# Token tiles shifted by 32 bytes in the partition, and three instead of four activation buffers in the down projection

## Chip, cores and metric

The kernel runs on one core of one Trainium2 chip. The metric is the device time of one execution in microseconds; of several executions the median counts.

## What is computed

A trunk of two layers over 256 tokens of width 1024. Each layer has a token mixer and then a retrieval over 16,384 single-neuron experts. The second part is what matters here:

```python
def peer_ffn(h, wq, keys, u_tab, v_tab):
    q = (h @ wq).reshape(b, s, PEER_HEADS, 2, PEER_HALF)
    sc = jnp.einsum('bshpd,hpnd->bshpn', q, keys)
    half_s, half_i = lax.top_k(sc, PEER_TOPK)
    ...
    gate = jax.nn.softmax(top_s, axis=-1)
        act = jax.nn.gelu(jnp.einsum('td,thkd->thk', hb, u_tab[eb]), approximate=False)
        return jnp.einsum('thk,thkd->td', gb * act, v_tab[eb])
```

The kernel does not gather the chosen experts. It computes the activations of all 16,384 experts (u, the up projection), multiplies them with a gate that is zero for experts not chosen, and multiplies the result with all of v (the down projection).

## The kernel before

**Products in parts.** Every fp32 operand is split into a high part (rounded to fp32r) and a low part (the rest), and a product is three matmuls: high by high, high by low, low by high.

**Weights.** All weight matrices pass through one stream (class `Stream`, lines 144 to 214) in pieces of 128 x 1024. A piece is loaded by SP into one of four `raw` tiles, and split in two halves of 512 columns into the rings `hi` and `lo` of three pieces. A split is of one of three kinds, chosen by shares that differ by stage: ACT rounds to `hi` (L199) and DVE subtracts to `lo` (L201); the same with POOL for the subtraction; or, the kind called dma here, ACT writes the negated rounding to `lo` (L195), POOL issues a DMA that adds `raw` onto it in memory (L196), and ACT writes `hi` (L197), all of it once for each half. A ring slot is written again when the matmuls of three pieces earlier have read it.

**Tokens.** The normalized tokens h stand in two tiles named `mid`, each 128 x (8 x 256) fp32r: `hhi` and `hlo`. `products` (L359 to L361, called for the query, up and some mixer projections) streams a 256-column row of them past 128 x 128 weights from `hi` and `lo`: 24 matmuls for one weight piece, 7,296 in the program (2,432 on each line). The up projection has 128 pieces in each layer. In the mixer's v, sv and su projections (L657 to L659) the roles are turned: a `mid` slice is the stationary operand, 192 matmuls in all. At three of the norms (`norm_mod`) the first four products run on another operand, `xparts`, which lies in a `big` tile: eight rows of 258 columns, one behind the other. The tile starts at a multiple of 64 bytes and a row is 1,032 bytes long, so row c starts 8c bytes past a multiple of 64, and row 4 starts 32 bytes past one. The 24 matmuls of a product go through the rows in order, three on each.

**Down.** `down` (L902) takes one v piece after another, chunk i of 128. `prep(i)` writes the high and low part of chunk i's activations into buffer i modulo 4 of a tile `ab` (ACT L910, DVE L911); then 12 matmuls (L925), with `ab` stationary and 512 columns of `hi` or `lo` moving. The third and fourth of them are the first to read `lo`: its first and its second half.

**Gates.** While up and down run, `gates` builds one-hot tiles `o1`, `o2`, `og` in fp16 and multiplies them (L876, 16 matmuls of 64 columns with `o1` stationary, 128 such groups); `o1` is stored to DRAM (`kept`) and read again.

**Order.** The program is written as a stream of work with a background scheduler that hands out slices by estimated costs; the framework then orders each engine's queue once more by data dependencies and buffers. In the course of the first layer's down projection DVE also runs 40 products with the next layer's modulation weights (L283), which wait for transfers of 512.5 KB (`wmod`).

The tiles `mid` and `xparts` are laid out by

```python
return self.one.tile([P, *shape], dt, name="mid", tag="mid", bufs=2)
n = NC * (T + 2)
self.xparts = [y[:, 8192 - (2 - i) * n:8192 - (1 - i) * n].rearrange("p (c t) -> p c t", c=NC) for i in range(2)]
```

Of the kernel before, what the change touches and what calls it, by code (L numbers as in the profile page):

```python
# [10 lines left out]
F32 = mybir.dt.float32  # L11
F32R = mybir.dt.float32r
# [6 lines left out]
P = 128  # L19
D = 1024  # L20
T = 256
# [195 lines left out]
class Trunk:  # L217
# [139 lines left out]
    def mm3(self, out, whi, wlo, hhi, hlo, start, stop):  # L357
        mm = self.nc.tensor.matmul
        mm(out, whi, hhi, start=start, stop=False)  # L359
        mm(out, whi, hlo, start=False, stop=False)  # L360
        mm(out, wlo, hhi, start=False, stop=stop)  # L361
# [539 lines left out]

    def down(self, acts):  # L902
        nc = self.nc
        ab = self.mid(4, 2, T, dt=F32R)
        self.acc = self.accs(4)

        def prep(i):
            src = acts[i // 32][:, i % 32]
            a = ab[:, i % 4]
            nc.scalar.activation(out=a[:, 0], in_=src, func=AF.Copy)  # L910
            nc.vector.tensor_tensor(out=a[:, 1], in0=src, in1=a[:, 0].bitcast(F32), op=ALU.subtract)  # L911

        for i in range(NK):
            if i % 64 == 0:
                prep(i)
                prep(i + 1)
            whi, wlo = self.weights()
            a = ab[:, i % 4]
            last = i == NK - 1
            terms = [(s, w, d) for s, w in ((0, whi), (0, wlo), (1, whi)) for d in range(2)]  # L920
            if last:
                terms.sort(key=lambda k: k[2])
            for tt in range(2):
                for s, w, d in terms:
                    nc.tensor.matmul(self.acc[2 * tt + d], a[:, s, P * tt:P * tt + P], w[:, 512 * d:512 * d + 512],  # L925
                                     start=i == 0 and s == 0 and w is whi, stop=last and s == 1)
            if i % 64 < 62:
                prep(i + 2)
            self.ahead()
            self.bg.pump(STEP)  # L930
            if i == 63:
                self.bg.finish()
                yield
        yield
# [83 lines left out]
    def start(self):  # L1018

        nc, io, one = self.nc, self.io, self.one  # L1020
        self.cols = one.tile([P, L * NCOL + 8], F32, name="cols")
        self.ident = one.tile([P, P], F32, name="ident")
        self.xT = one.tile([P, NC, T], F32, name="xT")
        self.ones = one.tile([P, P], F32, name="ones")
        self.eps = one.tile([P, 1], F32, name="eps")
        self.iota = one.tile([P, P, 2], FP16, name="iota")
        self.modT = one.tile([P, L, 48], F32, name="modT")
        self.idx = one.tile([P, 2, T], FP16, name="idx")
        self.gidx = one.tile([P, 2 * T], FP16, name="gidx")
        nc.vector.memset(self.ones, 1.0)  # L1030
        nc.vector.memset(self.eps, EPS)
        self.neghalf = one.tile([P, 8], F32, name="neghalf")
        nc.vector.memset(self.neghalf, -0.5)
        self.m = m = Carve(self.big(), self.big())
        self.m2 = Carve(self.big())
        row = m.take(D)
        nc.sync.dma_start(out=row[0:1], in_=io["crow"])
        nc.sync.dma_start(out=self.cols, in_=io["cols"])
        for i in range(2):
            nc.sync.dma_start(out=self.xT[:, 4 * i:4 * i + 4], in_=io["xT"][:, 4 * i:4 * i + 4])  # L1040
        cr = self.m2.take(D + 1)
        for i in range(2):
            b = self.bank()
            nc.tensor.matmul(b, self.ones[0:1], row[0:1, 512 * i:512 * i + 512], start=True, stop=True)
            nc.scalar.activation(out=cr[:, 512 * i:512 * i + 512], in_=b, func=AF.Silu)
        nc.vector.memset(cr[:, D:D + 1], 1.0)
        bufs = [self.m2.take(D + 1) for _ in range(6)]
        mods = self.mod_tiles(0, [j for c in range(NC) for j in (c, 8 + c)], cr, bufs, tail=False)
        next(mods)
        rs = self.rstd_d(m)  # L1050
        self.stream.depth = 0
        self.stream.share = {}
        self.stream.load(1)
        r = self.bias_rows()
        a = m.take(2, T)
        hhi, hlo = hb = [self.mid(NC, T, dt=F32R) for _ in range(2)]
        for c in range(NC):
            for _ in range(2 if c else 1):
                next(mods)
            sh, sc = self.modT[:, 0, c:c + 1], self.modT[:, 0, 8 + c:9 + c]  # L1060
            nc.vector.tensor_scalar(out=sc, in0=sc, scalar1=1.0, scalar2=self.col(0, c, 1), op0=ALU.add, op1=ALU.mult)
            t = a[:, c % 2]
            nc.vector.scalar_tensor_tensor(out=t, in0=self.xT[:, c], scalar=sc, in1=rs, op0=ALU.mult, op1=ALU.mult)
            nc.scalar.activation(out=hhi[:, c], in_=t, func=AF.Identity, bias=sh)  # L1064
            if c in (2, 4):
                self.stream.split(c // 2 - 1)
            nc.vector.scalar_tensor_tensor(out=hlo[:, c], in0=t, scalar=sh, in1=hhi[:, c].bitcast(F32), op0=ALU.add,  # L1067
                                           op1=ALU.subtract)
        for _ in mods:
            pass  # L1070
        self.stream.load(3)
        self.stream.depth = self.stream.RAW
        nc.sync.dma_start(out=self.ident, in_=io["consts"][:, 0:P])
        m.reset()
        self.bias = m.take(4, 256)
        self.table = self.bg.add(self.bias_table(r), rank=-1)
        self.bg.pump(0.1)
        self.mods = self.mod_tiles(0, list(range(16, 40)), cr, bufs[0:WBUFS])
        return hb
# [101 lines left out]
```

## Time and profile before

| | |
|---|---|
| median of 3 runs | 2026.73 us (2021.88 to 2034.16) |
| profiled execution, its own time | 2021.12 us |
| its span, first to last instruction | 2019.4 us |
| mean granted TensorE clock | 0.971 |
| PE busy | 1891.7 us (94%) |
| PEld (weight loads, beside PE) busy | 1711.1 us (85%) |
| DVE busy | 1472.8 us (73%) |
| ACT busy | 1130.2 us (56%) |
| POOL busy | 483.7 us (24%) |
| read from HBM | 388.72 MB |

Matmuls are pipelined and their ends are modelled, so the length of one in the trace is longer than the distance to the next. The distance from start to start is what is read here. A clock share of 1.00 is 2.4 GHz, 0.50 is 1.2 GHz.

### The profile page before, as it was taken

To read this page: it belongs to the slowest core of one execution; us is meant where nothing else is said; L and a number is where in the kernel's file an instruction comes from. 1 tells how busy PE (TensorE), PEld (TensorE's weight loads), DVE (VectorE), ACT (ScalarE), POOL (GpSimd) and SP (SyncE) were. 2 spreads that over 40 slices of the span, in tenths; PEclk is the share of its full clock that TensorE was granted. 3 is DMA by queue.
4 is the path that set the end of the run, shared out by engine and by line. 5 is a ranking of instruction groups with operands and counts; after the bars stand their busy time and mean duration, and the time that the engine had idled before them with its cause. 6 is when DMAs were issued, how large, how long until landed. Compare 5 with 4: busy or idle time off the path is not lost.

```text
span 2019.4 us, 37831 instructions
## 1 busy us (share of the span) xinstructions
PE 1891.7 (94%) x13718; PEld 1711.1 (85%) x13718; DVE 1472.8 (73%) x3360; ACT 1130.2 (56%) x2272; POOL 483.7 (24%) x432
## 2 busy tenths in 40 slices
PE   6887988999999999899998999998999999999998
PEld 4787988999999877678887899988999988888886
DVE  7888799677765887577668778954477668755555
ACT  4666543555555554455557676655555555565554
POOL 0122356751111111000001125877311111110001
PEclk7898998999999999899999999999999999999999
DMA  8987745767888888888557578887878888877674
GB/s 288 295 253 234 224 147 188 281 203 234 253 251 242 272 265 300 266 303 285 192 174 198 157 195 237 231 220 200 246 239 260 258 246 267 265 209 226 204 205 125
DMA packets 156958, 471.43 MB, mean 233 GB/s; under 512 B 17724, under 2 KB 19041, under 8 KB 156514
## 3 DMA queue, kind: packets, MB, share of 16 engines
q1 hardware_dynamic: 122786, 407.13, 58.7%
q0 software_dynamic: 33984, 61.88, 17.4%
q8 instruction: 107, 1.75, 0.3%
q14 instruction: 81, 0.66, 0.1%
HBM read 388.72 MB, written 18.36 MB: 202 GB/s over the span
## 4 chain that ended last, share of the span: by engine, by line
PE 63%; DMA 15%; DVE 11%; issue 6%; ACT 2%; POOL 2%; SPq 0%; POOLq 0%; DVEq 0%; ACTq 0%
PE acc L925 27%; PE bank L361 11%; PE bank L359 11%; PE bank L360 10%; DMA lo<-raw 10%; DMA big<-wmod 2%; DVE lo L201 2%; DMA raw<-v 2%; DVE big L283 2%; PE acc L876 1%; PE bank L876 1%; POOL lo L196 1%; DVE big L786 1%; POOL lo L201 1%; DVE big L787 1%
## 5 line engine op out<-in xcount | busy, mean ns | idle before, releaser
L199 ACT ACTIVATE hi<-raw 128x512 fp32r<-128x512 f32 x964 | 577.4, 624 | 366.3 <-PE bank L360 236.6
L361 PE MATMUL bank<-mid,lo 128*128 128x256 f32 x2432 | 700.2, 288 | 43.8 <-DMA lo<-raw 27.1
L359 PE MATMUL bank<-mid,hi 128*128 128x256 f32 x2432 | 702.5, 290 | 6.4 <-ACT mid L1064 5.9
L201 DVE TENSOR_TENSOR lo<-raw,hi 128x512 fp32r<-128x512 f32 x798 | 550.3, 714 | 212.5 <-ACT hi L199 207.6
L360 PE MATMUL bank<-mid,hi 128*128 128x256 f32 x2432 | 695.8, 286 | 0.8 <-DVE mid L1067 0.8
L925 PE MATMUL acc<-hi,mid 128*128 128x512 f32 x2048 | 570.3, 396 | 0.1
L361 PEld LDWEIGHTS bank<-mid,lo 128*128 128x128 f32 x2432 | 474.4, 195 | 51.9 <-DMA lo<-raw 31.6
L196 POOL DMA_DIRECT2D lo<-raw x236 | 203.9, 870 | 1175.5 <-ACT lo L195 851.1
L359 PEld LDWEIGHTS bank<-mid,hi 128*128 128x128 f32 x2432 | 473.4, 195 | 10.3 <-ACT mid L1064 7.0
L360 PEld LDWEIGHTS bank<-mid,hi 128*128 128x128 f32 x2432 | 474.2, 195 | 2.4 <-DVE mid L1067 2.0
L925 PEld LDWEIGHTS acc<-hi,mid 128*128 128x128 f32 x2048 | 386.2, 191 | 78.7 <-ACT mid L910 0.4
L925 PE MATMUL acc<-lo,mid 128*128 128x512 f32 x1024 | 326.0, 397 | 22.4 <-DMA lo<-raw 22.3
L201 POOL TENSOR_TENSOR lo<-raw,hi 128x512 fp32r<-128x512 f32 x166 | 261.8, 1652 | 97.5 <-ACT hi L199 88.7
L910 ACT ACTIVATE mid<-big 128x256 fp32r<-128x256 f32 x256 | 106.0, 416 | 303.1 <-PE acc L925 301.5
L925 PEld LDWEIGHTS acc<-lo,mid 128*128 128x128 f32 x1024 | 195.1, 191 | 71.9 <-DMA lo<-raw 31.0
L911 DVE TENSOR_TENSOR mid<-big,mid 128x256 fp32r<-128x256 f32 x256 | 107.9, 423 | 185.5 <-PE acc L925 144.5
L197 ACT ACTIVATE hi<-raw 128x512 fp32r<-128x512 f32 x236 | 147.5, 625 | 86.7 <-PE bank L360 54.9
L195 ACT ACTIVATE lo<-raw 128x512 fp32r<-128x512 f32 x236 | 146.6, 621 | 47.2 <-PE acc L925 44.7
L283 DVE SCALAR_TENSOR_TENSOR big<-big 128x1025 f32<-128x1025 f32 x96 | 122.3, 1281 | 35.0 <-DMA big<-wmod 26.8
L871 DVE TENSOR_TENSOR og<-o,gidx 128x512 f16<-128x512 f16 x256 | 96.5, 418 | 0.8 <-PE bank L876 0.4
L895 ACT ACTIVATE big<-bank 128x256 f32<-128x256 f32 x256 | 93.7, 366 | 0.0
L876 PEld LDWEIGHTS <-o 128*128 128x128 f16 x2048 | 67.3, 97 | 15.9 <-issue 13.1
(200 smaller groups left out, 1568.5 us busy)
## 6 DMA issues: line engine op xcount, KB each, us to landing
raw<-u SPq DMA_DIRECT2D x256, 512.0 KB, 4.8
raw<-v SPq DMA_DIRECT2D x256, 512.0 KB, 4.3
lo<-raw POOLq DMA_DIRECT2D x236, 256.0 KB, 5.1
big<-wmod SPq DMA_DIRECT2D x96, 512.5 KB, 6.4
raw<-win SPq DMA_DIRECT2D x40, 512.0 KB, 5.3
raw<-wq SPq DMA_DIRECT2D x32, 512.0 KB, 4.7
kept<-o SPq DMA_DIRECT2D x64, 256.0 KB, 4.9
o<-kept SPq DMA_DIRECT2D x64, 256.0 KB, 4.6
```

The lines of the kernel that those rows point to most:

```text
L195: nc.scalar.activation(out=lo, in_=raw, func=AF.Copy, scale=-1.0)
L196: nc.gpsimd.dma_start(out=lo, in_=raw, accum_op=ALU.add)
L197: nc.scalar.activation(out=hi, in_=raw, func=AF.Copy)
L199: nc.scalar.activation(out=hi, in_=raw, func=AF.Copy)
L201: eng.tensor_tensor(out=lo, in0=raw, in1=hi.bitcast(F32), op=ALU.subtract)
L283: nc.vector.scalar_tensor_tensor(out=w, in0=w, scalar=1.0, in1=sc, op0=ALU.mult, op1=ALU.mult, accum_out=self.modT[:, l, j:j + 1])
L359: mm(out, whi, hhi, start=start, stop=False)
L360: mm(out, whi, hlo, start=False, stop=False)
L361: mm(out, wlo, hhi, start=False, stop=stop)
L876: nc.tensor.matmul(b[:, 64 * j:64 * j + 64], o1[:, j // 2, :, j % 2], og[:, j // 2, s, :, j % 2], start=s == 0, stop=s == 1)
L911: nc.vector.tensor_tensor(out=a[:, 1], in0=src, in1=a[:, 0].bitcast(F32), op=ALU.subtract)
L925: nc.tensor.matmul(self.acc[2 * tt + d], a[:, s, P * tt:P * tt + P], w[:, 512 * d:512 * d + 512], start=i == 0 and s == 0 and w is whi, st ...
```

## The change

```diff
     def down(self, acts):
         nc = self.nc
-        ab = self.mid(4, 2, T, dt=F32R)
+        ab = self.mid(8 + 6 * T, dt=F32R)[:, 8:].rearrange("p (i s t) -> p i s t", i=3, s=2)
         self.acc = self.accs(4)
 
         def prep(i):
             src = acts[i // 32][:, i % 32]
-            a = ab[:, i % 4]
+            a = ab[:, i % 3]
...
             whi, wlo = self.weights()
-            a = ab[:, i % 4]
+            a = ab[:, i % 3]
...
         r = self.bias_rows()
         a = m.take(2, T)
+        one.tile([P, 8], F32, name="pad2")
         hhi, hlo = hb = [self.mid(NC, T, dt=F32R) for _ in range(2)]
```

`pad2` is never written or read. It is taken from the pool just before the first `mid` tile, and what is allocated later moves up by its 32 bytes a partition. In the built programs the two `mid` buffers go from bytes 201600 and 209792 of a partition to 201632 and 209824: from a multiple of 64 to 32 past one. `o1`, `o2` and `og` lie behind them and move in the same way (the first `o1` from 217984 to 218016). `hi`, `lo`, `raw`, `big` and all other tiles stay, at multiples of 64 for the four named. `ab` begins 8 words into its `mid` buffer, so that it is at a multiple of 64 again (201664 for the first), and has three buffers of 2 x 256 words instead of four.

With three buffers, `prep(i)` may write when the matmuls of chunk i - 3 have read, not those of chunk i - 4. The order on PE and POOL is the same in both programs. On ACT and DVE only rows of the down projection move, and on SP some loads of that time. The clearest place is a split of the dma kind. ACT before, at such a split in the second layer (`lo_64` and `hi_63` are the rings, `raw_21322` the piece, `mid` the tile of `ab`; names in brackets are semaphores of the engine or queue waited for):

```order
L910 ACTIVATE mid_18247<-big_15270 128x256 [waits PE_49]
L199 ACTIVATE hi_63<-raw_21302 128x512 [waits DMAHW6_49,DVE_49,PE_49]
L199 ACTIVATE hi_63<-raw_21302 128x512 [waits DVE_49,PE_49]
L195 ACTIVATE lo_64<-raw_21322 128x512 [waits DMAHW7_49,DVE_49,PE_49]
L197 ACTIVATE hi_63<-raw_21322 128x512 [waits PE_49,Activation_49]
L195 ACTIVATE lo_64<-raw_21322 128x512 [waits DVE_49]
L197 ACTIVATE hi_63<-raw_21322 128x512 [waits PE_49,Activation_49]
L910 ACTIVATE mid_18247<-big_15270 128x256
L910 ACTIVATE mid_18247<-big_15270 128x256 [waits PE_49]
```

ACT after, at the same split (the piece is now named `raw_21323`):

```order
L910 ACTIVATE mid_18248<-big_15271 128x256 [waits DVE_49,PE_49]
L199 ACTIVATE hi_63<-raw_21303 128x512 [waits DMAHW6_49,DVE_49,PE_49]
L199 ACTIVATE hi_63<-raw_21303 128x512 [waits DVE_49,PE_49]
L195 ACTIVATE lo_64<-raw_21323 128x512 [waits DMAHW7_49,DVE_49,PE_49]
L910 ACTIVATE mid_18248<-big_15271 128x256 [waits PE_49,Activation_49]
L197 ACTIVATE hi_63<-raw_21323 128x512 [waits PE_49,Activation_49]
L195 ACTIVATE lo_64<-raw_21323 128x512 [waits DVE_49]
L197 ACTIVATE hi_63<-raw_21323 128x512 [waits PE_49,Activation_49]
L910 ACTIVATE mid_18248<-big_15271 128x256 [waits DVE_49,PE_49]
```

A preparation that stood behind the whole split now stands between the first half's L195 and the second half's. This is so at 30 of the 32 dma splits of the two down projections.

DVE before, in the first layer's down projection where the modulation products (L283) run:

```order
L911 TENSOR_TENSOR mid_7446<-big_2081,mid_7446 128x256 [waits DVE_49,PE_49,Activation_49]
L283 SCALAR_TENSOR_TENSOR big_9589,modT_72<-big_9589 128x1025 [waits DMAHW1_49]
L201 TENSOR_TENSOR lo_64<-raw_9181,hi_63 128x512 [waits DMAHW6_49,Activation_49]
L201 TENSOR_TENSOR lo_64<-raw_9181,hi_63 128x512 [waits Activation_49]
L911 TENSOR_TENSOR mid_7446<-big_2081,mid_7446 128x256 [waits PE_49]
```

DVE after, at the same piece (now `raw_9182`):

```order
L283 SCALAR_TENSOR_TENSOR big_9590,modT_72<-big_9590 128x1025 [waits DMAHW7_49]
L291 SCALAR_TENSOR_TENSOR modT_72<-modT_72,cols_66 128x8
L911 TENSOR_TENSOR mid_7447<-big_2082,mid_7447 128x256 [waits PE_49,Activation_49]
L201 TENSOR_TENSOR lo_64<-raw_9182,hi_63 128x512 [waits DMAHW6_49,Activation_49]
L201 TENSOR_TENSOR lo_64<-raw_9182,hi_63 128x512 [waits Activation_49]
```

The preparation (L911) stood behind the split of a piece (L201, twice) and now stands ahead of it, and an L283, which waits for a transfer, is ahead of both.

## Rows read from the trace of the kernel before

**Rows 1.** The page's chain that ended last, shares of the span by line.
```profile
PE acc L925 27%; PE bank L361 11%; PE bank L359 11%; PE bank L360 10%; DMA lo<-raw 10%; DMA big<-wmod 2%; DVE lo L201 2%; DMA raw<-v 2%; DVE big L283 2%; PE acc L876 1%; PE bank L876 1%; POOL lo L196 1%; DVE big L786 1%; POOL lo L201 1%; DVE big L787 1%
```

**Rows 2.** By stage: length, busy us (count) of PE, PEld, DVE, ACT, POOL; clock; DMA; GB/s.
```profile
430.00:645.00 215.00, 213.59 (x2148) 211.75 (x2146) 142.59 (x295) 119.22 (x235) 33.86 (x37) 1.00 0.81 244
645.00:850.00 205.00, 187.44 (x1207) 148.71 (x1203) 157.74 (x350) 101.51 (x206) 20.64 (x24) 0.96 0.87 274
...
1400.00:1633.00 233.00, 230.19 (x2265) 228.47 (x2265) 142.87 (x299) 130.49 (x255) 49.39 (x51) 0.99 0.83 249
...
1800.00:2004.00 204.00, 202.68 (x888) 165.45 (x887) 113.03 (x200) 114.18 (x233) 14.32 (x17) 1.00 0.67 200
```

**Rows 3.** PE timeline, second layer's up: start us, length us, operation.
```profile
1451.82 0.65 PE L876 MATMUL acc<-og,o 128*128 128x64 f16 x16
1452.30 0.36 PE L359 MATMUL bank<-mid,hi 128*128 128x256 f32 x1
1452.50 0.28 PE L360 MATMUL bank<-mid,hi 128*128 128x256 f32 x1
...
1455.98 0.28 PE L359 MATMUL bank<-mid,hi 128*128 128x256 f32 x1
```

**Rows 4.** PE timeline, last product on `xparts` in the second layer's norm, and what follows.
```profile
1182.71 0.28 PE L359 MATMUL bank<-big,hi 128*128 128x258 f32 x1
...
1184.15 0.28 PE L359 MATMUL bank<-big,hi 128*128 128x258 f32 x1
...
1184.51 0.29 PE L359 MATMUL bank<-big,hi 128*128 128x258 f32 x1
...
1185.60 0.28 PE L359 MATMUL bank<-mid,hi 128*128 128x256 f32 x1
```

**Rows 5.** Groups by line, form and operation: busy us, mean ns | idle before.
```profile
L324 DVE SCALAR_TENSOR_TENSOR big<-xT,modT,big 128x256 fp32r<-128x256 f32 x24 | 12.9, 584 | 0.7 <-ACT big L323 0.6
...
L349 DVE SCALAR_TENSOR_TENSOR mid<-big,modT,mid 128x256 fp32r<-128x256 f32 x24 | 10.6, 482 | 1.8 <-ACT mid L348 1.5
```

**Rows 6.** ACT timeline at a dma split, second layer's down after its gates.
```profile
1821.67 0.42 ACT L910 ACTIVATE mid<-big 128x256 fp32r<-128x256 f32 x1 [1.26 <-PE acc L925]
1821.99 1.14 ACT L199 ACTIVATE hi<-raw 128x512 fp32r<-128x512 f32 x2
1824.16 0.63 ACT L195 ACTIVATE lo<-raw 128x512 fp32r<-128x512 f32 x1 [1.03 <-PE acc L925]
...
1825.22 0.62 ACT L195 ACTIVATE lo<-raw 128x512 fp32r<-128x512 f32 x1
```

**Rows 7.** POOL timeline: issue of that split's second half, and the last in the stage.
```profile
1826.13 0.86 POOL L196 DMA_DIRECT2D lo<-raw  x1 [0.18 <-issue]
...
1991.57 0.86 POOL L196 DMA_DIRECT2D lo<-raw  x1 [0.18 <-issue]
```

**Rows 8.** PE timeline there: two chunks' starts, and the wait for that half.
```profile
1818.75 1.07 PE L925 MATMUL acc<-hi,mid 128*128 128x512 f32 x4
...
1821.47 1.07 PE L925 MATMUL acc<-hi,mid 128*128 128x512 f32 x4
...
1831.18 0.50 PE L925 MATMUL acc<-lo,mid 128*128 128x512 f32 x1 [0.25 <-DMA lo<-raw]
```

**Rows 9.** PE's waits (us in total, times, longest): 760 to 870 us, then 1640 to 2000.
```profile
PE acc L925 <- DMA lo<-raw: 15.4, 11, 2.6
...
PE acc L925 <- DMA lo<-raw: 1.2, 4, 0.5
```

**Rows 10.** A piece of the chain in time order, first layer's down: start us, us.
```profile
824.28 8.55 DMA lo<-raw
```

**Rows 11.** Clock and PE timeline after a stall in the first layer's down.
```profile
814.40:816.50 2.10, 2.10 (x6) 1.65 (x5) 0.98 (x2) 0.00 (x0) 0.00 (x0) 0.50 0.67 185
...
814.42 1.91 PE L925 MATMUL acc<-hi,mid 128*128 128x512 f32 x4
816.13 0.91 PE L925 MATMUL acc<-lo,mid 128*128 128x512 f32 x2
```

## The prediction

> **What bounds the kernel now.** I read the chain of work that ended last first [rows 1]: the down matmuls hold 27% of it, the three lines of the token products 11, 11 and 10%, and the DMA that makes low parts 10%. The view by stage then says where PE sets the pace [rows 2]. In up it is busy 213.59 of 215 us and 230.19 of 233, so a nanosecond on each token matmul there is a nanosecond of the kernel. In the second layer's down it is 202.68 of 204. Only the first layer's down leaves PE idle for long, 187.44 of 205, with the DMA engines at a share of 0.87. So two things can move the time: the distance between PE's matmuls, and the waits in down.
>
> The distances come from the PE timelines, from start to start. A token matmul of 256 columns follows the last after 3.48 / 29 = 120.0 ns [rows 3]. A down matmul of 512 columns takes 2.72 / 12 = 226.7 ns [rows 8]. The 256 further columns cost 106.7 ns, so 13.3 ns of each fp32r matmul do not depend on its columns. All of it at a granted clock of 1.00, the level of 2.4 GHz.
>
> **Part 1: the moving operand of the token products at 32 past a multiple of 64.** There are 7,296 matmuls on L359, L360 and L361. The kernel before reads no `mid` row from such an address, but it reads `xparts` rows from eight offsets, the fifth of them exactly 32. One product of 24 such matmuls with 258 columns runs from 1182.71 to 1185.60 [rows 4], 120.4 ns each, where 120.0 and two columns at 0.417 ns would be 120.8. The three on row 4, at offset 32, take 0.36 us, 120 ns each. These reads also cross one boundary of 64 bytes more than an aligned row does, as the shifted tokens will, and pay nothing for it. I take 0 for this part. The average over the offsets is 0.4 ns below, which is 2.9 us over all; the three at offset 32 are read in steps of 10 ns, so 3 ns to either side of one, and 7,296 x 3 = 21.9 us is the bound in both directions.
>
> **Part 2: stationary operands at the new offset.** `o1` in the gates (2,048 matmuls, 0.48 us for 16, 30 ns each [rows 3]) and the 192 token slices of L657 to L659. No row of before shows a stationary operand of either type at offset 32. The nearest is the aligned one; I take 0, because 30 ns holds 26.7 for 64 columns and so little else that the load must lie beside other work. What it costs if it does not is the third rival. From below the bound is those 3.3 ns, 2,048 x 3.3 = 6.8 us. The Trainium skill ("TensorE: Matmul & The Clock Gate", section "Weight-path perf modes — Fast Weight Load (FWL) and DoubleRow") asks for 128 weights and a type other than FP32 for its fast load and names no address; by it nothing changes here either, and no run here shows it yet.
>
> **Part 3: writes of shifted tiles.** The low parts of tokens take DVE 482 ns each [rows 5]; the same operation into the shifting rows of `xparts` has a mean of 584. If all of that were the address, 32 operations (L349 24 times and 8 more in the first norm) would cost 32 x 0.10 = 3.3 us, on DVE, which has room. ACT's and DVE's work in down stays at its old offset. Stores and loads of `o1` start 32 bytes further on; their loads are issued a gate ahead. I take 0 for all of it.
>
> **Part 4: three buffers.** A preparation may now run two chunks ahead of its use, not three: 2 x 2.72 = 5.4 us [rows 8], of which it needs 0.42 on ACT and about as much on DVE. On plain chunks it stands where one stood before, ahead of the two L199 [rows 6]. That is covered. On DVE it now stands ahead of L201 and behind an L283 that waits for its transfer; that eats of the same 5.4 us, and is covered unless the transfer is some 4 us late.
>
> At 30 of the 32 dma splits it is not covered. The first half's L195 waits for the same matmul as before, so nothing is gained there. But the preparation now stands between it and the second half's L195, and ACT gives the next instruction 0.32 us after a preparation starts (1821.67 to 1821.99, [rows 6]). Queued behind it are L197, the second L195, POOL's second issue and the DMA. That L195 ends at 1825.84, POOL issues 0.29 us later [rows 6, 7], and the DMA lands just before 1831.18, where PE has waited 0.25 us for it [rows 8]. So this half comes 0.32 us later, and PE's wait becomes 0.57.
>
> How many of the 32 does it hit? The seven whose second halves are issued from 1826.13 to 1991.57 us [rows 7] have no gates to hide them: chunks of bare matmuls, and PE already waits at about half of them (four waits, 1.2 us, [rows 9]). 7 x 0.32 = 2.2 us. In the first layer, from 760 to 870 us, PE has 11 waits of 15.4 us together [rows 9], one or two at each of six splits; a second half takes up to 8.55 us to land there [rows 10] against 5.0 for the one in rows 7 and 8, so its bytes stand in full queues and a later start costs less than its delay. I take half, 6 x 0.16 = 1.0 us. The other 19 lie nearly all among gates, without such waits, and one gate's 0.48 us of PE time covers 0.32. Together 3.2 us; the ends are 0 and 32 x 0.32 = 10.2.
>
> **The sum.** 0 + 0 + 0 + 3.2 on the profiled execution's 2021.12 us (span 2019.4) gives 2024.3. That execution is 5.6 us below the median shown, so on the median it is 2026.7 + 3.2 = 2029.9 us, 0.2% slower. What a measurement of this kernel can tell from no change is about 0.5%, 10 us, so I call this no change.
>
> **The rivals.**
>
> *Faster: the shifted rows take away part of the 13.3 ns.* If the moving rows and the weights, both at multiples of 64 now, hold each other up at the change of weights, another offset frees it. Half of it is 7,296 x 6.65 = 48.5 us, 1978 us; all of it 97 us, 1930. For it speaks that the 13.3 ns is the same for 256 and 512 columns and so may belong to the change of weights, where both operands are read. Against it speak the three matmuls at offset 32 with 120 ns [rows 4]: half of the 13.3 would be 113. Chance 0.17. The Trainium skill (the same page, section "Back-to-back issue gap") gives N / 2.4 + 2.5 ns for a single matmul's gap, 109.2 ns for 256 columns; were that reached, an estimate from it is 10.8 x 7,296 = 79 us and a time of 1948. The trace disagrees with the formula for this type, by 120.0 to 109.2 here.
>
> *Slower: the late second half costs everywhere.* Place: the dma splits of both down projections. If the 19 others are as tight as the seven at the end, all 32 pay 0.32, 10.2 us. And a stall can lower the clock: after the one that ended just before 814.4 us the granted clock is 0.50, the level of 1.2 GHz, and matmuls follow after 1.71 / 4 = 0.43 us instead of 0.23 [rows 11]. If each of the first layer's six brings another 2.1 us at half clock, that is 6 x 1.05 = 6.3 more: 16.5 in all, 2043 us. It decides from the point where the cover among the gates is below 0.32 us. Against it: those splits show no wait now. Chance 0.13.
>
> *Slower: stationary operands at offset 32 load late.* If each pays a second time what an fp32r change of weights costs, 2,240 x 13.3 = 29.8 us, 2056.5. Nothing in the trace shows it, nothing excludes it. Chance 0.07.
>
> *The shift does nothing and the order neither:* the halves are late but land together with their neighbours. 2026.7 us, chance 0.05.
>
> **How the numbers follow.** The forecast has 0.58. Within it the time can be 2019 to 2041 (the spread of the runs of before, 4.9 below to 7.4 above, the 2.9 us of part 1 and the ends of part 4); of its chance I give 0.08 to slower by over 0.5% and 0.02 to faster. Faster: 0.15 of the first rival, whose small gains fall under no change, and 0.02, so 0.17. Slower: 0.13 + 0.07 + 0.08 = 0.28. Same: 0.55. The range is 2005 to 2046: it holds the forecast, the case without any effect, the first slower rival, and of the faster rival what lies within part 1's bound of 21.9 us; outside stay most of the faster rival and the loading of stationary operands.
>
> **What would show it.** Right: 120 ns between token matmuls in up, 30 ns in gates, and from 1826 us on a wait of PE at nearly every dma split, a third of a microsecond more than now, with ACT's second L195 0.32 us later behind the first. Wrong: any other distance in up, to either side (0.5 ns would be 3.6 us); gate groups of 16 that take other than 0.48 us; or new waits among the gates of down.

## The result, and the profile after

The changed kernel takes 2043.04 us (median of 19 runs, 2036.44 to 2055.50), the kernel before 2029.47 us beside it (19 runs). The ratio is 1.0064, 95% interval [1.0049, 1.0080]: 13 us slower. This lies in the range of the prediction, 2005 to 2046, but on its slower side; the likeliest case, no change by 0.5%, did not come.

The profiled execution of after has a span of 2039.4 us at a mean clock of 0.965, that of before 2019.4 at 0.971. Of these 20 us some 6 are chance: before was profiled 8 us below its own median, after 2 below. Single profiles are therefore read by distances and waits, not by their ends.

The first look is at the distance from matmul to matmul. PE timeline of after, second layer's up (start us, length us, operation), which answers to [rows 3]:

```profile
1453.54 0.28 PE L361 MATMUL bank<-mid,lo 128*128 128x256 f32 x1
...
1457.05 0.28 PE L361 MATMUL bank<-mid,lo 128*128 128x256 f32 x1
```

Thirty steps in 3.51 us are 117.0 ns, where [rows 3] had 120.0. The mean over all such steps of the trace is 117.3 (before: 119.9). The token products became faster. The same view in the second layer's down after its gates, which answers to [rows 8]:

```profile
1898.59 1.10 PE L925 MATMUL acc<-hi,mid 128*128 128x512 f32 x4
...
1901.39 1.10 PE L925 MATMUL acc<-hi,mid 128*128 128x512 f32 x4
```

One chunk of 12 matmuls takes 2.80 us, 233.3 ns each, against 2.72 and 226.7 in [rows 8]. The means over the whole traces are 233.3 and 227.3: 6.0 ns on each of 3,072 matmuls is 18.4 us of PE time. The down products became slower, and the prediction had no term for that.

By stage (length, busy us and count of PE, PEld, DVE, ACT, POOL; clock; DMA share; GB/s), which answers to [rows 2]:

```profile
430.00:645.00 215.00, 211.62 (x2148) 208.67 (x2147) 143.04 (x299) 120.40 (x239) 33.31 (x37) 1.00 0.82 248
645.00:850.00 205.00, 190.41 (x1192) 148.77 (x1191) 153.81 (x343) 98.31 (x198) 20.69 (x24) 0.94 0.84 267
1400.00:1633.00 233.00, 226.18 (x2245) 223.20 (x2244) 150.79 (x297) 128.97 (x255) 59.35 (x56) 0.99 0.82 245
1800.00:2004.00 204.00, 203.26 (x869) 162.72 (x868) 113.30 (x200) 113.68 (x234) 14.58 (x17) 1.00 0.70 209
```

In the second layer's up PE is busy for 4 us less of the same 233 us than in [rows 2], and in the bare chunks at the end it does 869 matmuls where it did 888. Where the 4 us went, the waits of PE tell (us in total, times, longest), second layer's up from 1230 us on, before:

```profile
PE bank L361 <- DMA lo<-raw: 12.6, 10, 2.5
```

and after:

```profile
PE bank L361 <- DMA lo<-raw: 17.9, 14, 3.6
```

PE now comes to some of the low parts before their DMA has landed: of the time that faster matmuls save, 5 us there turn into waiting in this pair of profiles. In down the same view after, first 760 to 870 us, then 1640 to 2000, answers to [rows 9]:

```profile
PE acc L925 <- DMA lo<-raw: 12.9, 10, 2.9
...
PE acc L925 <- DMA lo<-raw: 0.6, 1, 0.6
```

Both are lower than in [rows 9] (15.4 and 1.2). ACT at a dma split of the second layer's down, which answers to [rows 6]:

```profile
1826.51 0.63 ACT L195 ACTIVATE lo<-raw 128x512 fp32r<-128x512 f32 x1 [1.10 <-PE acc L925]
1827.05 0.40 ACT L910 ACTIVATE mid<-big 128x256 fp32r<-128x256 f32 x1
1827.35 0.61 ACT L197 ACTIVATE hi<-raw 128x512 fp32r<-128x512 f32 x1
1827.88 0.62 ACT L195 ACTIVATE lo<-raw 128x512 fp32r<-128x512 f32 x1
```

The preparation stands between the two L195, and the second begins 1.37 us after the first, 0.31 more than in [rows 6]. So the order moved as it was read from the program, but at the end of the kernel no wait grew from it.

### The profile page after: what moved, and what is told of

It reads as the page before. It is cut to its first block, busy times and chain, and to the rows that moved or that the text cites. A ratio compares the mean times of both kernels' runs of the same rounds, so it can differ in the third digit from the quotient of the medians.

```text
span 2039.4 us, 38042 instructions
## 1 busy us (share of the span) xinstructions
PE 1903.7 (93%) x13718; PEld 1703.8 (84%) x13718; DVE 1473.2 (72%) x3360; ACT 1128.4 (55%) x2272; POOL 482.8 (24%) x432
## 5 line engine op out<-in xcount | busy, mean ns | idle before, releaser
L201 DVE TENSOR_TENSOR lo<-raw,hi 128x512 fp32r<-128x512 f32 x798 | 549.1, 713 | 192.7 <-ACT hi L199 189.3
L925 PE MATMUL acc<-hi,mid 128*128 128x512 f32 x2048 | 582.3, 402 | 0.1
L361 PEld LDWEIGHTS bank<-mid,lo 128*128 128x128 f32 x2432 | 469.2, 193 | 59.1 <-DMA lo<-raw 36.8
L359 PEld LDWEIGHTS bank<-mid,hi 128*128 128x128 f32 x2432 | 468.7, 193 | 10.4 <-ACT mid L1065 7.1
L360 PEld LDWEIGHTS bank<-mid,hi 128*128 128x128 f32 x2432 | 469.4, 193 | 2.4 <-DVE mid L1068 2.0
L925 PE MATMUL acc<-lo,mid 128*128 128x512 f32 x1024 | 331.4, 403 | 21.0 <-DMA lo<-raw 20.8
L201 POOL TENSOR_TENSOR lo<-raw,hi 128x512 fp32r<-128x512 f32 x166 | 259.8, 1635 | 101.4 <-ACT hi L199 86.6
L911 DVE TENSOR_TENSOR mid<-big,mid 128x256 fp32r<-128x256 f32 x256 | 108.4, 424 | 226.1 <-PE acc L925 199.6
L195 ACT ACTIVATE lo<-raw 128x512 fp32r<-128x512 f32 x236 | 146.7, 622 | 50.9 <-PE acc L925 46.8
L283 DVE SCALAR_TENSOR_TENSOR big<-big 128x1025 f32<-128x1025 f32 x96 | 121.2, 1269 | 30.3 <-DMA big<-wmod 30.3
```

What stands on the lines that cost most here:

```text
L195: nc.scalar.activation(out=lo, in_=raw, func=AF.Copy, scale=-1.0)
L201: eng.tensor_tensor(out=lo, in0=raw, in1=hi.bitcast(F32), op=ALU.subtract)
L283: nc.vector.scalar_tensor_tensor(out=w, in0=w, scalar=1.0, in1=sc, op0=ALU.mult, op1=ALU.mult, accum_out=self.modT[:, l, j:j + 1])
```

## The experiments

Three things changed at once: the tokens' place, the place of `ab`, and the order that three buffers bring. The experiments take them apart. Starts of operands are given modulo 256 bytes; `hi` and `lo` start at 128 in the kernels before and after. The tokens start at 128 before and 160 after; `ab` at 128 before and 192 after. A term that the prediction called "a multiple of 64 again" is thus a change of place.

All kernels at a glance, distances as means over the whole traces:

```
kernel                              tokens  ab    256 columns  512 columns   us      ratio [95%]
before                              128     128   119.9 ns     227.3 ns      2029.5  1
after                               160     192   117.3        233.3         2043.0  1.0064 [1.0049, 1.0080]
e1 three buffers alone              128     128   119.9        227.3         2034.8  1.0041 [1.0022, 1.0060]
e2 and ab at 192                    128     192   119.9        233.2         2047.6  1.0105 [1.0078, 1.0132]
e3 after, ab at 0                   160     0     117.1        232.9         2040.3  1.0061 [1.0038, 1.0084]
e4 shift, four buffers              160     160   117.1        233.3         2040.4  1.0066 [1.0045, 1.0088]
e5 after, ab at 128                 160     128   117.2        227.6         2035.1  1.0021 [1.0003, 1.0039]
e6 before, weights shifted too      160     160   119.9        227.3         2033.0  1.0008 [0.9992, 1.0024]
e7 tokens at 192, ab at 128         192     128   117.6        227.5         2032.2  1.0010 [0.9991, 1.0030]
e8 e1, preparation after split      128     128   119.9        227.3         2031.0  0.9992 [0.9970, 1.0015]
e9 e5, preparation after split      160     128   117.1        227.4         2026.1  0.9982 [0.9963, 1.0001]
e10 e7, preparation after split     192     128   117.6        227.4         2027.8  0.9989 [0.9970, 1.0009]
```

In e6 alone `hi` and `lo` start at 160. Each ratio is to runs of before beside it on the same chip (medians 2028.9 for e1 to e4, 2031.2 for e5 to e8, 2029.4 for e9 to e11).

**Three buffers alone.** Before, with three buffers and nothing moved:

```diff
-        ab = self.mid(4, 2, T, dt=F32R)
+        ab = self.mid(3, 2, T, dt=F32R)
...
-            a = ab[:, i % 4]
+            a = ab[:, i % 3]
```

> The kernel before with three activation buffers in down, at the old addresses: no shift of the token tiles, ab at a multiple of 128 bytes. In the traces a down matmul of 512 columns follows the last after 226.7 ns before and 233.3 ns after the change; 3,072 of them make 20 us. Theory A (address): the stationary operand's start modulo 128 sets this distance, and the change moved it from 0 to 64. Then it stays 226.7 here, and the time is that of before plus what the later second halves of the dma splits cost: 0 to 10 us, 3 expected. Theory B (buffers): the shorter lead or the new order of ACT and DVE slows the matmuls. Then it is 233.3 here as well and the time is 13 to 23 us above before.

Measured 2034.77 us, 1.0041 [1.0022, 1.0060], 8 us slower with every distance as before: theory B is out. Buffers and order cost more than the 3.2 us of the sum.

**The place of `ab` alone.** As e1, with `ab` 16 words into its tile, at 192 as in the changed kernel:

```diff
-        ab = self.mid(4, 2, T, dt=F32R)
+        ab = self.mid(16 + 6 * T, dt=F32R)[:, 16:].rearrange("p (i s t) -> p i s t", i=3, s=2)
```

> As the first run, but ab starts 64 bytes further on (a multiple of 64, not of 128); token tiles at their old place. Theory A: 233.3 ns in down, 120 ns in up, some 15 to 23 us above before. Theory B: the same distance as in the first run, whatever that is, and the same time.

PE timeline of this kernel, two starts one chunk apart:

```profile
1903.20 1.10 PE L925 MATMUL acc<-hi,mid 128*128 128x512 f32 x4
...
1906.00 1.10 PE L925 MATMUL acc<-hi,mid 128*128 128x512 f32 x4
```

Again 2.80 us, 233.3 ns, now with unshifted tokens. The time is 2047.64 us, 1.0105 [1.0078, 1.0132]: 13 us above e1, whose only difference is the place of `ab`. So the slow down matmuls come from there, and the changed kernel, with the same `ab` and the same order, is 8 us below this one by the ratios (1.0105 to 1.0064): that is what its faster token products give.

**`ab` at a multiple of 256.** After, with `ab` at 0:

```diff
-        ab = self.mid(8 + 6 * T, dt=F32R)[:, 8:].rearrange("p (i s t) -> p i s t", i=3, s=2)
+        ab = self.mid(24 + 6 * T, dt=F32R)[:, 24:].rearrange("p (i s t) -> p i s t", i=3, s=2)
```

> The changed kernel with ab 24 words instead of 8 into its tile: token tiles stay at 32 past a multiple of 64, ab is at a multiple of 128 again. Theory A: 226.7 ns in down; token matmuls of up keep the 117.3 ns that the changed kernel shows against 119.9 before. 6,144 x 2.6 ns = 16 us if PE alone set the pace of up, but up took as long in the changed kernel as before, so between 10 us below and 3 us above before. Theory B: 233.3 ns and the time of the changed kernel, 13 us above before.

It measured 2040.33 us with 232.9 ns in down: as slow as at 192. Theory A with its modulus of 128 is out as well. A start at a round address is not what helps: before's 128 is better than 0, which cannot be a matter of alignment alone.

**The shift without the buffers.** Before, with only the line `one.tile([P, 8], F32, name="pad2")` added: four buffers, order as before, `ab` at 160 like the tokens.

> The shift alone: pad2 is there, ab has four buffers at the start of its tile, so it too lies 32 past a multiple of 128. Theory A: the distance in down is not 226.7; 233 or more, and the time at least 8 us above before. If only the half of 128 matters it could be anything between. Theory B: four buffers and the old order, 226.7 ns, and the time of before or a little below.

It measured 2040.44 us, 1.0066 [1.0045, 1.0088], 117.1 ns in up and 233.3 in down. The place 160 costs down as much as 192 and 0 do. That left two readings: down wants `ab` at 128, or it wants `ab` where the weights are.

**`ab` back at 128.** After, with `ab` 56 words into its tile:

```diff
-        ab = self.mid(8 + 6 * T, dt=F32R)[:, 8:].rearrange("p (i s t) -> p i s t", i=3, s=2)
+        ab = self.mid(56 + 6 * T, dt=F32R)[:, 56:].rearrange("p (i s t) -> p i s t", i=3, s=2)
```

> The changed kernel with ab 56 words into its tile. Modulo 256 bytes, hi and lo start at 128; so far a start of ab at 128 gave 227.3 ns in down (before, and the first run), 192, 0 and 160 gave 233.2, 232.9 and 233.3. Here ab is at 128 of 256 again while the token tiles keep their shift of 32. Theory C: the distance depends on the starts modulo 256, and is short in down when both operands have the same. Then 227 ns in down, 117 in up; the time is that of the three buffers alone (8 us above before) less what up gives back, at most 16 us and so far some 8: between 6 us below before and 4 above. Theory D: a larger modulus, or something else in the shifted layout; then 233 ns in down and the time of the changed kernel, 13 us above.

PE timeline, two starts one chunk apart:

```profile
1900.40 1.07 PE L925 MATMUL acc<-hi,mid 128*128 128x512 f32 x4
...
1903.12 1.07 PE L925 MATMUL acc<-hi,mid 128*128 128x512 f32 x4
```

2.72 us as in before, and 2035.13 us, 1.0021 [1.0003, 1.0039]: about 9 us less than the changed kernel, for 48 words of address. Against before this is 4 us slower, the upper end of what was expected.

**Everything at 160.** Before, with eight words ahead of the weights' rings, so that weights, tokens and `ab` all start at 160 (line numbers behind it are one higher):

```diff
+        pool.tile([P, 8], F32, name="pad0")
```

> The kernel before with 8 unused words ahead of hi and lo: every tile moves by 32 bytes, so hi, lo, the token tiles and ab all start at 160 of 256. If the difference between stationary and moving operand counts (theory C), nothing changes: 120 ns in up, 227 in down, the time of before within 5 us. If the address itself counts, against boundaries in the partition, up goes to about 117 and down to 233, and the time is up to 13 us above before.

PE timeline, up and then down:

```profile
1460.02 0.28 PE L360 MATMUL bank<-mid,hi 128*128 128x256 f32 x1
...
1463.62 0.28 PE L360 MATMUL bank<-mid,hi 128*128 128x256 f32 x1
...
1894.44 1.07 PE L926 MATMUL acc<-hi,mid 128*128 128x512 f32 x4
...
1897.16 1.07 PE L926 MATMUL acc<-hi,mid 128*128 128x512 f32 x4
```

Thirty steps in 3.60 us, 120.0 ns, and 2.72 us a chunk, 226.7: both as in before, to the tenth of a nanosecond in the means. Tokens at 160 are fast in e4 and slow here, and `ab` at 160 is slow in e4 and fast here. The two kernels differ only in where the weights, and the tiles laid out between them and the tokens, lie. The distance therefore depends on how the two operands of a matmul lie to each other, and not on the address of either.

**Tokens 64 bytes away.** After with a pad of 16 words, tokens at 192, `ab` at 128:

```diff
-        ab = self.mid(8 + 6 * T, dt=F32R)[:, 8:].rearrange("p (i s t) -> p i s t", i=3, s=2)
+        ab = self.mid(48 + 6 * T, dt=F32R)[:, 48:].rearrange("p (i s t) -> p i s t", i=3, s=2)
...
-        one.tile([P, 8], F32, name="pad2")
+        one.tile([P, 16], F32, name="pad2")
```

> Token tiles moved by 64 bytes instead of 32 (192 of 256), ab at 128 of 256, three buffers. By theory C any difference speeds up the token matmuls: 117 ns as at 32, and the time of the run with 32. If only an odd multiple of 32 does (two reads of one 64-byte piece), 120 ns and the time of three buffers alone, 8 us above before. Down 227 ns by theory C.

117.6 ns in up, and 2032.22 us: 64 bytes from the weights do nearly what 32 do. A crossing of a 64-byte boundary is not the cause, since the tokens here start at a multiple of 64.

**The order alone.** As e1, with the preparation written behind the split that the same chunk triggers:

```diff
+            self.ahead()
             if i % 64 < 62:
                 prep(i + 2)
-            self.ahead()
```

> As the first run (three buffers, old addresses), but prep(i + 2) is written after the split of that turn, so that ACT again has L195, L197, L195, L197 in a row at the dma splits and the preparation behind them. If the 8 us of the first run (2034.8 against 2028.9, 1.0041) come from the second half's late L195, as forecast, the time goes back to that of before within 3 us. If they come from the shorter lead of the preparations, they stay or grow.

ACT at a dma split in e1:

```profile
1820.34 0.63 ACT L195 ACTIVATE lo<-raw 128x512 fp32r<-128x512 f32 x1 [1.03 <-PE acc L925]
1820.88 0.40 ACT L910 ACTIVATE mid<-big 128x256 fp32r<-128x256 f32 x1
1821.19 0.62 ACT L197 ACTIVATE hi<-raw 128x512 fp32r<-128x512 f32 x1
1821.71 0.62 ACT L195 ACTIVATE lo<-raw 128x512 fp32r<-128x512 f32 x1
```

and in e8:

```profile
1819.64 0.63 ACT L195 ACTIVATE lo<-raw 128x512 fp32r<-128x512 f32 x1 [1.03 <-PE acc L925]
1820.17 0.62 ACT L197 ACTIVATE hi<-raw 128x512 fp32r<-128x512 f32 x1
1820.69 0.62 ACT L195 ACTIVATE lo<-raw 128x512 fp32r<-128x512 f32 x1
```

From first to second half 1.37 us in e1, 1.05 in e8. The time goes back to 2030.97 us, 0.9992 [0.9970, 1.0015], with three buffers still there. So three buffers alone cost nothing that these runs can tell, and the order costs the 8 us. That the late second half does it is not shown: the edit also puts some twenty preparations on DVE (L911) in the first layer behind a split's L201 that they stood ahead of in e1, and no run separates the two.

Where, the length of each down projection shows. PE's down matmuls of the first layer, first and last start (durations shortest, median, longest in ns; first to last start in us), in before:

```profile
L925 PE MATMUL acc<-hi,mid x1024: 387/389/628, 645.3 to 1048.8; 128*128 128x512 f32 x171
```

in e1:

```profile
L925 PE MATMUL acc<-hi,mid x1024: 387/389/628, 646.5 to 1052.8; 128*128 128x512 f32 x171
```

in e8:

```profile
L925 PE MATMUL acc<-hi,mid x1024: 387/390/632, 648.1 to 1049.6; 128*128 128x512 f32 x171
```

The stage takes 403.5, 406.3 and 401.5 us. Over the kernels whose down matmuls take 227 ns: with the preparation between the halves 406.3, 413.1 and 408.4 (e1, e5, e7), without 403.5, 401.2, 402.0, 401.5, 402.3 and 400.6 (before, e6, e11, e8, e9, e10). In the second layer all nine lie between 368.9 and 371.8. So the first layer pays. Cut into 40 equal windows, its 7.4 us between the means of the two groups divide into 3.0 us more in which PE is idle (24.4 against 21.4) and 4.0 us more lost to the clock (window by window, length times what the granted clock lacks to 1.00: 15.4 against 11.4). Stretches at half clock follow long waits, as [rows 11] showed.

Which waits grew, PE's timeline tells, since the third and fourth matmul of a chunk are the first to read the two halves of `lo`. One dma split of e1 in the first layer's down:

```profile
853.36 0.51 PE L925 MATMUL acc<-lo,mid 128*128 128x512 f32 x1 [1.96 <-DMA lo<-raw]
854.62 0.80 PE L925 MATMUL acc<-lo,mid 128*128 128x512 f32 x1 [0.76 <-DMA lo<-raw]
855.21 1.91 PE L925 MATMUL acc<-hi,mid 128*128 128x512 f32 x4
```

The first line waits for the first half, the second for the second half, and the third runs at a granted clock of 0.50 (1.91 us for four). Added up over the stage, the waits for second halves are shorter with the preparation between the halves (7.4 us on average in e1, e5 and e7, 9.9 in the six others), and those for first halves are longer (15.6 against 11.2); waits for a DVE low part (L201) go from 0.2 to 1.1. At the seven splits at which PE waits for most of this, the first half is issued 0.92 us after its L195 in both groups, but lands 7.8 us after the issue instead of 7.2. So what grew is not the wait for the delayed half. Why the first half takes longer to land is open.

**Both repairs.** e5 and e7 with the order of e8; e9 is e5 with that edit:

> Both gains together: token tiles shifted by 32 bytes, ab at 128 of 256 (as hi and lo), three buffers, and the preparation written after the split. The version with the shift alone stood at 1.0021, and writing the preparation after the split was worth 0.5% there (1.0041 to 0.9992). If the two add, 0.997 to 0.999, 2 to 6 us below before, 117 ns in up and 227 in down. If what up gives back goes into PE's waits for the splits, the time is that of before.

and e10 is e7 with it:

> The same with the token tiles shifted by 64 bytes: 117.6 ns in up. If the two add, 0.996 to 0.998 (1.0010 with the preparation ahead of the split); otherwise the time of before.

2026.07 us, 0.9982 [0.9963, 1.0001], and 2027.82, 0.9989 [0.9970, 1.0009]. Both are far below the changed kernel, by some 17 and 15 us; e9 is 8 us below e5 and e10 4 us below e7 by the ratios, the price of the order a second and a third time. The ratio of e10 stays short of the 0.996 to 0.998 that was expected. Against before neither can be told from no change: the 2.6 ns of each token matmul bring 3 us or nothing.

**What row 4 of `xparts` would have said.** Part 1 took its 0 from a row of `xparts` at offset 32. This kernel is before with 256 of the 258 columns read there, so that of columns and start only the start differs from a token product. Modulo 256, row c of the high part starts at 8c and of the low part at 64 + 8c, and the weights at 128: no row starts where the weights do.

```diff
-        first = self.products((xhi, xlo), 2, T + 2, stat)
+        first = self.products((xhi[:, :, 0:T], xlo[:, :, 0:T]), 2, T, stat)
```

> The kernel before, where the four first products of each norm read 256 of the 258 columns of an xparts row; the bias products in the last two columns are left out (a wrong column stands in for them). The rows keep their eight offsets. The forecast read 120.4 ns for 258 columns as proof that offsets cost and give nothing. If the two columns hid a gain (a row of 258 does not end where one of 256 does), the mean distance is now 117 to 118.5 ns; if the eight offsets really give nothing, 119.6 to 120.

PE timeline, row 4 of the last product and the first matmul of row 5:

```profile
1186.70 0.28 PE L359 MATMUL bank<-big,hi 128*128 128x256 f32 x1
...
1187.05 0.28 PE L359 MATMUL bank<-big,hi 128*128 128x256 f32 x1
```

0.35 us for three, where [rows 4] had 0.36. Means over all products are finer. Within row 4, the 258 columns of before take 120.6 ns (25 steps; 119.9 to 120.8 in the other kernels), the 256 columns 117.4 (20 steps, without one of 141 ns ahead of a pause). Two columns should cost 0.8 ns, and here they cost 3. So at equal columns row 4 comes close to the fast distance, and 258 columns hid it.

Over all eight rows the mean falls only from 120.4 to 119.4, which neither theory expected; row 4 was picked with the result in view, from one profile. The other rows limit the finding (14 to 27 steps each): rows 0 and 2 take 118.6 and 118.4 ns, rows 1, 3 and 5 take 120.8, 120.3 and 121.1, and rows 6 and 7 take 119.4 and 119.2. All of them start elsewhere than the weights, so a different start alone does not bring the fast distance. The one run of this kernel took 2031.22 us, too few for a time.

## Why the prediction was right and wrong

**Part 1, the moving tokens: wrong by the row it rested on.** The term was 0 and came out as a gain of 2.6 ns on each matmul, inside the bound of 3 ns. The step that failed is the reading of [rows 4]: three matmuls of 120 ns at offset 32 were taken as proof that the offset does nothing, after 0.8 ns for two columns. But the columns differed as well, and at equal columns the row takes 117.4 (e11). Nor was its place that of the shifted tokens: they start 32 bytes from the weights modulo 256, row 4 starts 160 and 224 bytes from them. The faster rival named the place, the interplay of the moving rows and the weights; of its 13.3 ns a fifth came, not half. Nor are the 13.3 ns a fixed part of every matmul: with differing starts the same subtraction, 2 x 117.2 - 233.2, leaves 1.2. The gain became little time: 6,144 matmuls of the two ups x 2.6 ns are 16 us, and 8 came back between e2 and the changed kernel, 4 between e1 and e5, 2 between e8 and e9. Over all profiles the two ups together take 826 us on the average with the slow distance (821 to 831, six kernels) and 821 with the fast one (820 to 822, seven), a gain of 5. In the same profiles PE is idle in the ups for 38.4 us with the fast distance and 33.1 with the slow one, and 13.4 against 10.5 are lost to the clock, so idle time took 5 of the 16, the clock 3, and some 3 are not accounted for. "A nanosecond on each token matmul there is a nanosecond of the kernel" was too strong: PE had almost no idle time in up, but the DMA of the low parts stood close behind it.

**Part 2, stationary operands: right in time for those it named, and the one that mattered was not named.** The gates keep their 30.7 ns with `o1` at the new place; PE groups by form, after:

```profile
L876 PE MATMUL bank<-og,o 128*128 128x64 f16 x1024 | 40.3, 194 | 0.0
```

(before: the same 40.3 us.) But `og`, the moving operand, moved along by the same 32 bytes, so in no kernel here do the two start differently, and the 0 for the gates is not tested beyond that. The token slices of L657 to L659 do change. Before and after, groups by form (busy us, mean ns):

```profile
L657 PE MATMUL acc<-hi,mid 128*128 128x512 f32 x32 | 12.5, 390 | 0.0
```

```profile
L657 PE MATMUL acc<-hi,mid 128*128 128x512 f32 x32 | 12.7, 396 | 0.0
```

From start to start that is 227.7 to 233.2 ns with 512 columns, and 119.7 to 118.6 with 256; on 96 matmuls of each, half a microsecond. The third rival asked for 13.3 ns more on 2,240 matmuls and a time of 2056.5; it was right that a stationary operand's place can cost and wrong on which, how much and why.

The step that failed here is "`ab` begins 8 words into its `mid` buffer, so that it is at a multiple of 64 again", carried into part 3 as "ACT's and DVE's work in down stays at its old offset". It looked at the address modulo 64 and at the engines that write `ab`, never at the matmuls that read it. [Rows 8] were used as a ruler for the other parts and not as a term: 3,072 matmuls, the largest group on the chain in [rows 1], went without a price because the tile seemed not to move. It moved from 128 to 192. This term is worth 13 us (e1 to e2), 9 us (after to e5), of 18.4 on paper.

**Part 3, the writes: right.** The low parts of tokens (L349, [rows 5]) take DVE 483 ns after, 482 before; the price of 584 did not come.

**Part 4, the order: right that it costs; its size, its place and its path were not.** The second half comes late as forecast, 0.31 us. The order costs some 8 us (e1), and writing the preparation behind the split takes back 10, 8 and 4 us in three pairs (e1 and e8, e5 and e9, e7 and e10; each known to about 6 us), where the term was 3.2. Its larger share, 2.2 us, was put on the bare chunks at the end. There e1 waits 1.9 us from 1640 to 2016 and e8 also 1.9, so nothing came of it. In the first layer, where 1.0 us was expected because "its bytes stand in full queues", 7.4 us appear. The step that failed there is "so this half comes 0.32 us later, and PE's wait becomes 0.57", which left the first half as it was: the waits for second halves shrank by 2.5 us and those for first halves grew by 4.4. The sentence that a stall can lower the clock stood in the slower rival with [rows 11], at 6.3 us, and 4.0 are seen. That rival's 2043 us is the median measured, but by coincidence: it held no term for `ab`, which is the larger part, and none for the gain in up. In the same way the range held the result in part by luck: its upper end was drawn for the late halves, and the largest part of the loss came from a term that the sum did not have.

**The sum as it came out.** Order 8, `ab` 13, tokens -8 by the chain e1, e2, after: 13 us. The parts do not add along every path: the shift with four buffers (e4), which lacks the order's 8 us, measures 1.0066 where after measures 1.0064. The intervals leave about 5 us to either side there. Part of it shows in the lengths of the first layer's down: where its matmuls are slow, the order adds 4 us (408.0 in e4; 412.2 to 412.6 in after, e2 and e3; one profile each), where they are fast 7.4. What else makes e4 as slow as after was not found.

**The size of the measurement.** The forecast had 0.55 for no change by 0.5%, because three terms of four were 0. The zero for the tokens was argued from a nearest row and came out as -8 us by one pair of runs. The largest piece, +13 us, was no zero but a missing term. Each was larger than the term that was worked out.

## What to carry to other kernels

When a tile moves, list every instruction that reads it and compare its start with that of the *other* operand, not with a round number: here the price hung on the difference. A nearest row proves no effect only if nothing but the thing in question differs in it; two more columns were enough to hide one. And where a preparation slips between the two halves of a split that feeds a DMA, try it behind the split: here that took back 4 to 10 us. To learn which wait a new order lengthens, add up the waits by what each matmul reads.

## What the runs showed of the hardware

For fp32r matmuls with 128 x 128 weights at full clock, the distance from start to start depends on where stationary and moving operand start relative to each other, modulo 256 bytes. If they start equal, 256 columns take 119.9 ns and 512 columns 227.3. With a difference of 32 or 64 bytes the token products of 256 columns take 117.1 to 117.6, and with one of 32, 64 or 128 bytes 512 columns take 232.9 to 233.3. Equal starts help the long ones by 6 ns and hurt the short ones by 2.6. Other differences are not covered by this: in e11 rows 1, 3 and 5 of `xparts`, which start 8, 24 and 40 bytes past a multiple of 64 where the weights start at one, take 120.3 to 121.1 ns with 256 columns.

The sign goes with the columns and not with the role of the token tile. In L657 to L659 tokens are stationary as `ab` is in down; with 512 columns they pay like down, with 256 columns they gain: 119.7 to 118.6 ns with 32 bytes of difference, 115.7 and 114.9 with 64 (e7, e10). The period is not 128, since `ab` at 0 with weights at 128 is slow (e3). It need not be longer than 256: `hi` starts at byte 16512 and `ab` at 201600 in before, at 201856 in e5, which differ from `hi` by 256 and by 0 modulo 512, and both are fast. The fp16 gates with 64 columns stay at 30.7 ns, with both operands moved alike. Why the sign turns between 256 and 512 columns is open; no run here looks inside the engine.

For a single matmul the Trainium skill ("TensorE: Matmul & The Clock Gate", section "Back-to-back issue gap") gives N / 2.4 + 2.5 ns, 109.2 and 215.8 ns for these two sizes. No placement tried here comes nearer than 114.9 (L657 to L659 in e10) and 227.3, so more than half of the surplus of this type stayed at every placement.
